# HGRN levels of a hybrid streaming encoder on one core: the masked copy bound behind both scalings, the first level's queries read side by side, one early pair's fourth weight sum on VectorE

## The chip, the cores and the metric

The kernel runs on one core of a Trainium2 chip. The metric is the device time of one execution, in microseconds, and the median over several runs is compared. A profile is of one execution, with times counted from the start of its span. The engines are named as the profile names them: PE (TensorE, matmuls, with PEld for its weight loads), DVE (VectorE), ACT (ScalarE), POOL (GpSimd) and SP (SyncE, which here only starts DMAs).

## The reference, cut to what matters

One inference step of one encoder layer, for 512 prompt frames and 32 frames of a running stream. A projection `proj = xn @ w_in` feeds two branches, an mLSTM with four heads and an HGRN2 with eight, and both are merged by gates and projected out. The change lies in the HGRN2 branch and in the projection that is computed beside it:

```
a = jnp.einsum('bhtc,bhtsc,bhsc->bhts', q, dec, k)      # dec = exp(g_t - g_s) for s <= t, per channel
o = jnp.einsum('bhtc,bhce->bhte', q * jnp.exp(g), S) + jnp.einsum('bhts,bhse->bhte', a, v)
```

The decay `dec` differs by channel c, so a plain matmul of q and k doesn't give `a`. The kernel computes it in levels.

## The kernel before

The frames are 544 columns (32 of the stream and 512 of the prompt), the 128 partitions are channels. The matrix products of the whole kernel are done by PE in three passes of rounded high and low parts, so each weight piece is cast by ACT (helper line L131) and its remainder is taken by DVE (L132). The projection's units come in pairs (class `Two`): seven products of 128x512 weight pieces and sums of pieces, in the manner of Strassen, in place of eight. The sums `s1`, `s2`, `s3`, `s4` of an early pair are made partly by DMAs that add into the tile (`s1`, `s3` in `begin`, L418 and L419, and `s4`, L476, all adding DMAs on POOL's queue), partly by DVE (L464). All sums `s1`, `s2`, `s4` of a pair live in one tile, called `ws` in the profile.

PE's order is written by hand: `Pump` hands out the pair products in steps of six matmuls (L501, tiles `d`), and `chain(h)`, which computes one HGRN head, says after each of its own pieces how many such steps follow (`STEPS`, 3 for most levels). The orders of DVE, ACT and POOL come from the tile framework's scheduler, which places each instruction by priority and by when it expects its inputs. Each engine then works its list strictly in order.

A head has seven levels, c = 1, 2, 4, ... 64. Tile `hkq` holds the head's keys `kk` and its queries `qq` side by side. At each level:

- ACT copies keys into `km`, a single buffer (L1640, later L1642), and for c under 16 saves some columns in `snap`.
- PE multiplies: two fp32 matmuls of 128 columns each into the PSUM tile `pl` (L1651, four instructions in the profile), at c = 16 three more columns' groups (L1659, L1661). The moving operand is read by `view`: runs of c columns, alternating between two places that are 288 + c columns apart.
- DVE scales half of the keys and half of the queries in place by decay products, in two instructions (L1675): the first scaling covers one half of the columns, the second the other. It then makes the next level's decay products (L1678, L1681) and copies the level's scores into `at` where a mask says so (L1682, COPY_PREDICATED).

The next level's `km` copy reads what the two scalings wrote, and the next level's matmuls read `km`. Nothing reads `at` before the head's last level is done.

Of the kernel before, what the change touches and what calls it, by code (L numbers as in the profile page):

```python
# [14 lines left out]
ALU = mybir.AluOpType  # L15
AX = mybir.AxisListType

P = 128
# [48 lines left out]
def hybrid_step(ctx: ExitStack, tc: tile.TileContext, a, o):  # L67
# [1442 lines left out]
    def view(t, off, dims):  # L1510
        base = t[:, 0:T]
        return bass.AP(base.tensor, base.offset + off, [list(base.ap[0])] + [list(d) for d in dims])
# [7 lines left out]
    def units():  # L1520


        def both(h):

            if "both" not in hs[h]:
                t = sp.tile([P, 2, SLOT], F32, tag="d", name=f"hkq{h}", bufs=2)
                hs[h].update(both=(t[:, 0], t[:, 1]), pair=t)
            return hs[h]["both"]

        def forget(h, raw):  # L1530
            lbc, lcc = lb[:, h : h + 1], lc[:, h : h + 1]
            tf, kk = eslot(f"tf{h}"), both(h)[0]
            for t, sign in ((tf, 1.0), (kk, -1.0)):
                S.activation(unrev(t), raw[:, :HB], AF.Sigmoid, scale=sign)
                S.activation(t[:, HB:T], raw[:, HB:T], AF.Sigmoid, scale=sign)
            S.activation(tf[:, :T], tf[:, :T], AF.Identity, scale=lcc, bias=lbc)
            S.mul(kk[:, :T], kk[:, :T], lcc)
            hs[h].update(tf=tf, kk=kk, kq=raw)

        def query(h, qq):  # L1540
            tf, kk, kq = (hs[h][k] for k in ("tf", "kk", "kq"))
            q0 = eslot(f"q0{h}")

            S.activation(unrev(q0), qq[:, :HB], AF.Sigmoid)
            S.activation(q0[:, HB:T], qq[:, HB:T], AF.Sigmoid)
            V.tensor_tensor(unrev(q0), unrev(q0), qq[:, :HB], ALU.mult)
            V.tensor_tensor(q0[:, HB:T], q0[:, HB:T], qq[:, HB:T], ALU.mult)
            V.tensor_tensor(qq[:, :T], q0[:, :T], tf[:, :T], ALU.mult)
            V.tensor_tensor(kq[:, :T], q0[:, :T], kk[:, :T], ALU.mult)
            hs[h].update(q0=q0, qq=qq)  # L1550

        def behind(h, then, t):

            if h:
                then(h, t)
            else:
                later.append(lambda: then(h, t))

        def value_tile(h):

            t = eslot(f"hi{h}")
            return t, (
                ((t[:, HB - 1 : HB - 1 - TH : -1], slice(0, TH)),),
                ((t[:, HB - 1 - TH :: -1], slice(0, HB - TH)), (t[:, HB:T], slice(HB - TH, TH))),
            )

        def value(h, t):
            hs[h]["ii"] = t

        def gate(h, t):  # L1570
            sg = slot(f"sg{h}")
            S.activation(sg[:, :T], t[:, :T], AF.Sigmoid)
            V.tensor_tensor(t[:, :T], t[:, :T], sg[:, :T], ALU.mult)
            hs[h]["gg"] = t

        def merge_a(f, t):
            gated[f] = S.activation(t[:, :T], t[:, :T], AF.Sigmoid)
            y = slot(f"ya{f}")[:, :T]
            nc.sync.dma_start(y, ya_d[f])
            V.tensor_tensor(y, y, t[:, :T], ALU.mult)  # L1580
            yas[f] = y

        def merge_b(f, t):
            S.activation(t[:, :T], t[:, :T], AF.Sigmoid)
            gbs[f] = t

        for h in range(HH):
            yield Two(
                [
                    (("q", h), 48 + h, lambda h=h: plain(both(h)[1]), lambda t, h=h: behind(h, query, t)),  # L1590
                    (
                        ("f", h),
                        56 + h,
                        lambda h=h: plain((slot if h else eslot)(f"kq{h}")),
                        lambda t, h=h: behind(h, forget, t),
                    ),
                ],
                h > 0,
                h == 0,
            )  # L1600
            yield Two(
                [
                    (("g", h), 72 + h, lambda h=h: plain(eslot(f"hg{h}")), lambda t, h=h: gate(h, t)),
                    (("i", h), 64 + h, lambda h=h: value_tile(h), lambda t, h=h: value(h, t)),
                ],
                True,
            )
        for f in range(0, KD, 2):
            for e in (
                pair("ga", f, 80 + f, lambda f: plain(eslot(f"ga{f}")), merge_a, True),  # L1610
                pair("gb", f, 88 + f, lambda f: plain(eslot(f"gb{f}")), merge_b, True),
            ):
                e.alone = True
                yield e
# [8 lines left out]
    def chain(h):  # L1623
# [10 lines left out]
        for li, c in enumerate(LEVELS):  # L1634
            smp = li == QUADS
            n = HB if smp else NA
            km = tp.tile([P, NA], F32, tag="vs", name=f"km{h}{c}", bufs=1)
            pump.behind = held[-1] if held else None
            with tc.high_priority():
                low = S.copy(  # L1640
                    km.rearrange("p (n j c) -> p n j c", j=2, c=c),
                    view(kk, HB, ((2 * c, NA // (2 * c)), (c - HB, 2), (1, c))),  # L1642
                )
                if li < QUADS:
                    S.copy(snap[:, :, li], hs[h]["pair"][:, :, csmp])
            held.append(low)
            yield STEPS[li]

            pn = paux(f"pl{h}{c}")
            for b in range(2):  # L1650
                PE.matmul(  # L1651
                    pn[:, 0, b * P : (b + 1) * P],
                    km[:, b * P : (b + 1) * P],
                    view(qq, b * P, ((2 * c, P // (2 * c)), (HB + c, 2), (1, c))),
                    start=True,
                    stop=True,
                )
            if smp:
                PE.matmul(pn[:, 0, NA:HB], kk[:, NA : NA + P], qq[:, csmp], start=True, stop=True)  # L1659
                ks, qs = (snap[:, i].rearrange("p l t -> p (l t)") for i in range(2))  # L1660
                PE.matmul(pn[:, 1, :P], ks, qs, start=True, stop=True)  # L1661
            nb, na = (HB if c < NS else NA) // (2 * c), NA // (2 * c)
            tb, ta = told[:, : 2 * nb], told[:, told.shape[-1] - 2 * na :]
            tn = ttmp[:, base : base + nb + na]
            sides = ((tb, 0, nb, 1, 0), (ta, HB, na, 0, nb))
            with tc.high_priority():
                for t, lo, m, first, _ in sides:

                    x = view(
                        kk, lo + first * c, ((qoff + (1 - 2 * first) * c, 2), (2 * c, m), (1, c))  # L1670
                    )
                    d = bass.AP(
                        t.tensor, t.offset + 1 - first, [list(t.ap[0]), [2 * first - 1, 2], [2, m], [0, c]]
                    )
                    V.tensor_tensor(x, x, d, ALU.mult)  # L1675
                if told.shape[-1] == 2 * (nb + na):
                    t = told.rearrange("p (n t) -> p n t", t=2)
                    V.tensor_tensor(tn, t[:, :, 0], t[:, :, 1], ALU.mult)  # L1678
                else:
                    for t, _, m, _, o_ in sides:  # L1680
                        V.tensor_tensor(tn[:, o_ : o_ + m], t[:, ::2], t[:, 1::2], ALU.mult)  # L1681
                V.copy_predicated(at[:, :n], lmask[:, li, :n], pn[:, 0, :n])  # L1682
                if smp:
                    for i in range(QUADS):
                        d = slice(i * NS, (i + 1) * NS)
                        V.copy_predicated(at[d, NA:HB], smask[d], pn[d, 1, d])
            base += nb + na
            if c == NS // 2:
                tsmp = tn[:, nb - 1 : nb]
            told = tn  # L1690
            if li == 0:

                yield 1
                pn = paux(f"pd{h}")
                for b, c_ in enumerate([c_ for c_, _, _ in chunks] + [slice(NA, NA + P)]):
                    PE.transpose(pn[:, b // NB, b % NB * P : (b % NB + 1) * P], kq[:, c_], ident)
                with tc.high_priority():
                    V.tensor_reduce(
                        dg, pn.rearrange("p a t -> p (a t)")[:, : 5 * P].rearrange("p (b t) -> p b t", t=P), AX.X, ALU.add
                    )  # L1700
            if li == (4 if h < HH - 1 else 6) and h:
                yield 1
                finish(h - 1)
# [328 lines left out]
```

## Time and profile before

| | |
|---|---|
| median of 3 runs | 1122.6 us (1119.49 to 1123.89) |
| the profiled execution: time, span | 1120.93 us, 1119.0 us |
| PE busy, PEld busy | 1108.0 us (99%), 1085.5 us (97%) |
| DVE busy, ACT busy, POOL busy | 896.4 us (80%), 669.9 us (60%), 167.8 us (15%) |
| granted TensorE clock | 1.000 |
| the HGRN heads' levels | 635.8 to 871.4 us |
| from one head's first level to the next one's | 30.7 us (729.41 to 760.09) |
| level matmuls, L1651 | 224 instructions, 37.8 us |
| level scalings L1675; masked copies L1682; km copies L1640 | 96 records, 40.7 us; 56, 25.2 us; 56, 24.0 us |

A row of the timeline has the start, the duration, the engine, the line, the instruction with its tiles, and in brackets the idle time in front of it with what ended that. Neighbours on one engine overlap a little in the records: the next DVE instruction starts some 0.08 us before the end that is shown for the one ahead, so a time from start to start is what an instruction costs its engine.

### The profile page before, as it was taken

To read this page: it belongs to the slowest core of one execution; us is meant where nothing else is said; L and a number is where in the kernel's file an instruction comes from. 1 tells how busy PE (TensorE), PEld (TensorE's weight loads), DVE (VectorE), ACT (ScalarE), POOL (GpSimd) and SP (SyncE) were. 2 spreads that over 40 slices of the span, in tenths; PEclk is the share of its full clock that TensorE was granted. 3 is DMA by queue.
4 is the path that set the end of the run, shared out by engine and by line. 5 is a ranking of instruction groups with operands and counts; after the bars stand their busy time and mean duration, and the time that the engine had idled before them with its cause. 6 is when DMAs were issued, how large, how long until landed. Compare 5 with 4: busy or idle time off the path is not lost.

```text
span 1119.0 us, 23773 instructions
## 1 busy us (share of the span) xinstructions
PE 1108.0 (99%) x8733; PEld 1085.5 (97%) x8733; DVE 896.4 (80%) x2040; ACT 669.9 (60%) x1506; POOL 167.8 (15%) x308
## 2 busy tenths in 40 slices
PE   9999999999999999999999999999999999999998
PEld 9889999999999999999999999999999999999998
DVE  6898988676896786976888699999999977654485
ACT  6767446754666555664655476777676667333462
POOL 7223010100020000200010123232222210000000
PEclk9999999999999999999999999999999999999999
DMA  6133314332353133541767655666665684332743
GB/s 230 57 113 118 124 57 163 117 95 96 128 175 141 57 119 124 164 164 60 240 166 252 179 133 133 147 137 144 150 157 144 160 223 157 109 105 71 263 153 118
DMA packets 90139, 157.94 MB, mean 141 GB/s; under 512 B 10148, under 2 KB 17828, under 8 KB 90024
## 3 DMA queue, kind: packets, MB, share of 16 engines
q1 hardware_dynamic: 80352, 139.33, 37.8%
q0 software_dynamic: 8784, 15.99, 9.0%
q8 instruction: 68, 1.11, 0.4%
q10 hardware_dynamic: 888, 1.12, 0.3%
q14 instruction: 47, 0.39, 0.1%
HBM read 131.49 MB, written 24.91 MB: 140 GB/s over the span
## 4 chain that ended last, share of the span: by engine, by line
PE 92%; DVE 4%; DMA 1%; ACT 1%; issue 1%; SPq 0%; POOL 0%; ACTq 0%; POOLq 0%; DVEq 0%
PE d L501 36%; PE ya L166 9%; PE pg L1879 4%; PE yb L166 4%; PE q L166 4%; PE o L166 4%; PE C L927 4%; PE k L166 4%; PE sc L887 3%; PE nm L1102 3%; PE pl L1651 2%; PE u L286 2%; PE vp L1410 2%; PE ple L166 1%; PE d L386 1%; DMA ws<-in_w_in 1%
## 5 line engine op out<-in xcount | busy, mean ns | idle before, releaser
L419 POOL DMA_DIRECT2D ws<-in_w_in x46 | 40.4, 884 | 228.4 <-DVE hkq L1675 22.2
L515 ACT COPY t<-d 128x272 f32<-128x272 f32 x126 | 47.7, 379 | 8.8 <-PE d L501 8.7
L1675 DVE TENSOR_TENSOR hkq<-hkq,q 128x288 f32<-128x288 f32 (+1 forms) x96 | 40.7, 430 | 2.5 <-PE pl L1659 0.9
L1651 PE MATMUL pl<-hkq,km 128*128 128x128 f32 x224 | 37.8, 291 | 1.3 <-ACT km L1640 1.1
L650 DVE SCALAR_TENSOR_TENSOR cv<-ub,vec,cv 128x547 f32<-128x547 f32 x48 | 37.5, 782 | 0.4
L1651 PEld LDWEIGHTS pl<-hkq,km 128*128 128x128 f32 x224 | 31.2, 189 | 3.0 <-ACT km L1640 2.7
L1640 ACT COPY km<-hkq 128x256 f32<-128x256 f32 x56 | 24.0, 428 | 16.5 <-DVE hkq L1675 7.4
L1036 DVE SCALAR_TENSOR_TENSOR c<-c,wi,Cs 128x258 f32<-128x258 f32 x32 | 15.3, 479 | 18.5 <-PE Cs L1034 18.1
L939 ACT COPY Co<-C 128x258 f32<-128x258 f32 x30 | 9.8, 378 | 30.7 <-PE C L927 28.4
L1187 DVE TENSOR_TENSOR y<-ya,y 128x272 f32<-128x272 f32 x48 | 18.8, 433 | 8.8 <-PE ya L166 8.7
L1682 DVE COPY_PREDICATED at<-lmask,pl 128x256 f32<-128x256 uint8 (+1 forms) x56 | 25.2, 449 | 0.1
L1113 ACT COPY y<-nm 128x516 f32<-128x516 f32 x16 | 9.4, 590 | 22.7 <-PE nm L1102 22.6
L642 POOL COPY uo<-ub 128x3 f32<-128x3 f32 x16 | 17.5, 1092 | 34.5 <-DVE ub L524 26.5
L476 POOL DMA_DIRECT2D ws<-in_w_in x15 | 15.5, 1032 | 33.9 <-DVE ws272l L132 24.9
L1619 POOL TENSOR_SCALAR_AFFINE_SELECT aa<-at 128x128 f32<-128x128 f32 x32 | 19.2, 682 | 8.0 <-DVE at L1682 8.0
L1090 DVE BATCH_NORM_STATS2 bs<-y 128x6 f32<-128x512 f32 (+1 forms) x20 | 13.8, 690 | 8.0 <-ACT y L1113 7.8
L826 POOL COPY vsm<-vt 128x96 f32<-128x96 f32 x12 | 6.2, 515 | 88.9 <-DVE vt L522 45.4
L1102 PE MATMUL nm<-vhl,sh 128*128 128x258 f32 x112 | 18.4, 286 | 0.6 <-ACT y L1113 0.6
L1866 DVE TENSOR_TENSOR h<-o,h 128x272 f32<-128x272 f32 x16 | 6.3, 436 | 14.5 <-PE o L166 14.5
L1781 ACT ACTIVATE osq<-kq 128x128 f32<-128x128 f32 x32 | 9.8, 305 | 12.4 <-DVE kq L1776 12.1
L901 ACT CAST sh<-dm 128x512 fp32r<-128x512 f32 (+3 forms) x16 | 7.3, 458 | 16.3 <-DVE dm L895 16.3
L1102 PEld LDWEIGHTS nm<-vhl,sh 128*128 128x128 f32 x112 | 15.4, 190 | 1.2 <-ACT y L1113 0.8
(4498 smaller groups left out, 4985.2 us busy)
## 6 DMA issues: line engine op xcount, KB each, us to landing
ws<-in_w_in POOLq DMA_DIRECT2D x61, 256.0 KB, 4.6
ws<-in_w_in SPq DMA_DIRECT2D x46, 256.0 KB, 3.5
ya_d<-y SPq DMA_DIRECT2D x32, 272.0 KB, 2.3
y<-ya_d SPq DMA_DIRECT2D x24, 272.0 KB, 3.8
c<-in_C SPq DMA_DIRECT2D x16, 258.0 KB, 3.6
out_Cs<-c SPq DMA_DIRECT2D x16, 258.0 KB, 2.7
out_Cp<-Co SPq DMA_DIRECT2D x12, 258.0 KB, 2.5
x<-in_xT SPq DMA_DIRECT2D x8, 272.5 KB, 5.1
```

The source lines that it names most:

```text
L166: PE.matmul(both[b][:m, :TH], part(w, off + k * step, m, x), xx[:, half(b)], start=(k == 0 and j == 0), stop=(k == n - 1 and j == 2),)
L419: G.dma_start(t, w_in[u][:, i * WP : (i + 1) * WP], accum_op=ALU.add)
L501: PE.matmul(ps, ww[:, c], xx, start=(start and k == 0 and j == 0), stop=end, skip_group_check=not start,)
L515: self.kept = S.copy(t, ps)
L650: V.scalar_tensor_tensor(cv[:, :547], ub[:, j : j + 547], vcol(V_CW + 4 * ft + j), cv[:, :547], ALU.mult, ALU.add)
L887: PE.matmul(pn[:, 0, :n], ks[f][x][:, j * P : (j + 1) * P], qs[f][y][:, NS + j * P : T], start=(f == 0 and i == 0), stop=(f == KH - 1 and ...
L927: PE.matmul(pn[g][:, :VH], kw[b][x][:, f * P : (f + 1) * P], vv[b][y][:, g * VH : (g + 1) * VH], start=(b == 0 and j == 0), stop=(b == NB ...
L1102: PE.matmul(pn[:, g, :VH], st[j][x][:, (i - j) * P : (i - j + 1) * P], vv[j][y][:, g * VH : (g + 1) * VH], start=(j == 0 and q == 0), stop ...
L1651: PE.matmul(pn[:, 0, b * P : (b + 1) * P], km[:, b * P : (b + 1) * P], view(qq, b * P, ((2 * c, P // (2 * c)), (HB + c, 2), (1, c))), star ...
L1675: V.tensor_tensor(x, x, d, ALU.mult)
L1682: V.copy_predicated(at[:, :n], lmask[:, li, :n], pn[:, 0, :n])
L1879: PE.matmul(ps, part(w, k * P, P, x), xx[:, c], start=(k == 0 and j == 0), stop=(k == KD - 1 and j == 2))
```

## The change

It has three parts. In `units()`, the first pair of head 1 (queries and forget gate, units 49 and 57) gets `alone = True`, by which its fourth sum `s4` is made by a DVE addition (L464) and not by an adding DMA from POOL (L476). In `chain(h)`, at the level c = 1, the moving operand is read as 64 columns two apart in one place and then 64 two apart in the other, and the result is written into `pl` two columns apart, so that it stands in the same order as before. And the masked copy L1682 gets an ordering edge behind the level's second scaling.

```
@@ units()
-            yield Two(
+            first = Two(
...
                 h > 0,
                 h == 0,
             )
+            first.alone = h == 1
+            yield first
@@ chain(h)
             for b in range(2):
-                PE.matmul(
-                    pn[:, 0, b * P : (b + 1) * P],
-                    km[:, b * P : (b + 1) * P],
-                    view(qq, b * P, ((2 * c, P // (2 * c)), (HB + c, 2), (1, c))),
-                    start=True,
-                    stop=True,
-                )
+                out, dims = pn[:, 0, b * P : (b + 1) * P], ((2 * c, P // (2 * c)), (HB + c, 2), (1, c))
+                if c == 1:
+                    out, dims = out.rearrange("p (i s) -> p s i", s=2), (dims[1], dims[0])
+                PE.matmul(out, km[:, b * P : (b + 1) * P], view(qq, b * P, dims), start=True, stop=True)
...
-                    V.tensor_tensor(x, x, d, ALU.mult)
+                    scaled = V.tensor_tensor(x, x, d, ALU.mult)
...
-                V.copy_predicated(at[:, :n], lmask[:, li, :n], pn[:, 0, :n])
+                with tc.issue_after(scaled.ins):
+                    V.copy_predicated(at[:, :n], lmask[:, li, :n], pn[:, 0, :n])
```

PE's list stays as it was, but for the form of the c = 1 matmuls. DVE's and ACT's lists are laid out anew by the scheduler through all eight heads. The profile's lines of the unchanged code shift by one or two: the scaling L1675 becomes L1674, the `km` copy L1640 becomes L1642, `snap` L1645 becomes L1647, L1678 becomes L1677.

DVE, head 3, level c = 4 (`pl_10491` is its score tile, `hkq_9773` the head's keys and queries, `ws_10272` the sum tile of a gate pair in the pump, L524 and L183 other work). Before:

```order
L524 SCALAR_TENSOR_TENSOR kq_10248<-d_10246,t_10474 128x272
L1675 TENSOR_TENSOR hkq_9773<-hkq_9773,q_10123 128x2x36x4
L1682 COPY_PREDICATED at_10364<-lmask,pl_10491 128x256
L1675 TENSOR_TENSOR hkq_9773<-hkq_9773,q_10123 128x2x32x4
L183 SCALAR_TENSOR_TENSOR rsq_u<-rsq_u,hv 128x5
L464 TENSOR_TENSOR ws_10272<-ws_10272,wi76r_9982 128x512
```

The same place in the changed kernel:

```order
L524 SCALAR_TENSOR_TENSOR kq_10248<-d_10246,t_10474 128x272
L1674 TENSOR_TENSOR hkq_9773<-hkq_9773,q_10123 128x2x36x4
L183 SCALAR_TENSOR_TENSOR rsq_u<-rsq_u,hv 128x5
L464 TENSOR_TENSOR ws_10272<-ws_10272,wi76r_9982 128x512
L1674 TENSOR_TENSOR hkq_9773<-hkq_9773,q_10123 128x2x32x4
L1682 COPY_PREDICATED at_10364<-lmask,pl_10491 128x256
```

The masked copy has left the place between the two scalings, and a five-column step and a weight sum of 128x512 have taken it. At this level the heads 1 to 7 read alike.

ACT, head 3, from the `km` copy of c = 8 (`km_10498`) to that of c = 16 (`km_10545`); `ws276h` is the cast of the sum that L464 made. Before:

```order
L1640 COPY km_10498<-hkq_9773 128x256
L1645 COPY snap<-hkq_9773 128x2x32
L131 CAST ws276h<-ws_10272 128x512
L1535 ACTIVATE tf_10560<-kq_10248 128x256
L131 CAST ws376h<-ws_10275 128x512
L1640 COPY km_10545<-hkq_9773 128x256
L526 ACTIVATE kq_10248<-d_10245 128x272
```

The same stretch in the changed kernel:

```order
L131 CAST ws276h<-ws_10272 128x512
L1642 COPY km_10498<-hkq_9773 128x256
L1647 COPY snap<-hkq_9773 128x2x32
L131 CAST ws376h<-ws_10275 128x512
L1535 ACTIVATE tf_10560<-kq_10248 128x256
L526 ACTIVATE kq_10248<-d_10245 128x272
L1642 COPY km_10545<-hkq_9773 128x256
```

The `km` copy of c = 8 now stands behind the cast of the sum, and that of c = 16 behind L526, which reads a pair product that PE must have finished.

DVE, head 3, level c = 32 (`pl_10647`); L1548 and L1549 make the next head's queries. Before:

```order
L1548 TENSOR_TENSOR hkq_10247<-q_10597,tf_10560 128x544
L1675 TENSOR_TENSOR hkq_9773<-hkq_9773,q_10123 128x2x4x32
L1682 COPY_PREDICATED at_10364<-lmask,pl_10647 128x256
L1675 TENSOR_TENSOR hkq_9773<-hkq_9773,q_10123 128x2x4x32
L1549 TENSOR_TENSOR kq_10248<-q_10597,hkq_10247 128x544
```

And in the changed kernel:

```order
L1548 TENSOR_TENSOR hkq_10247<-q_10597,tf_10560 128x544
L1674 TENSOR_TENSOR hkq_9773<-hkq_9773,q_10123 128x2x4x32
L1549 TENSOR_TENSOR kq_10248<-q_10597,hkq_10247 128x544
L1674 TENSOR_TENSOR hkq_9773<-hkq_9773,q_10123 128x2x4x32
L1677 TENSOR_TENSOR q_10597<-tf_10560 128x272
L1682 COPY_PREDICATED at_10364<-lmask,pl_10647 128x256
```

Here the 544-column product L1549 stands between the scalings. So it is in the heads 1 to 6.

## The prediction

> **What bounds the kernel now.** I read the page first: the engines' shares and the chain.
>
> ```profile
> PE 1108.0 (99%) x8733; PEld 1085.5 (97%) x8733; DVE 896.4 (80%) x2040; ACT 669.9 (60%) x1506; POOL 167.8 (15%) x308
> PE 92%; DVE 4%; DMA 1%; ACT 1%; issue 1%; SPq 0%; POOL 0%; ACTq 0%; POOLq 0%; DVEq 0%
> ```
>
> PE is busy for 99% of the span and carries 92% of the chain. Only two things can move the end: what PE itself does, and the moments when it waits. DVE at 80% looks harmless, but the change lies in one stage, so next come the windows there (columns: length, then busy us of PE, PEld, DVE, ACT, POOL).
>
> ```profile
> 700.00:800.00 100.00, 100.00 (x811) 99.22 (x810) 97.45 (x277) 72.10 (x203) 28.46 (x40) 1.00 0.65 149
> ```
>
> Among the HGRN heads PE is full and DVE too, at 97%: a list of work in strict order with hardly a gap. What is put ahead of something there delays it by its full length. The waits of PE for the `km` copies, from the view of waits, say how much there is to win:
>
> ```profile
> PEld pl L1651 <- ACT km L1640: 2.7, 6, 0.9
> ```
>
> Six waits, 2.7 us in all. Together with a cheaper first level (below, at most 1.8 us) the whole change has some 4.5 us to win, 0.4% of the time. Differences within 0.5% (5.6 us) are about what the measurement can't tell from none, so a clear gain is nearly excluded from the start.
>
> **The first level's queries.** The timeline of PE in head 3: the level matmuls of c = 1, c = 2 and c = 32, each with the next two matmuls.
>
> ```profile
> 729.41 0.83 PE L1651 MATMUL pl<-hkq,km 128*128 128x128 f32 x4
> 729.94 0.43 PE L501 MATMUL d<-xfh,ws252h 128*128 128x272 f32 x1
> 730.21 0.29 PE L501 MATMUL d<-xfl,ws252h 128*128 128x272 f32 x1
> ...
> 733.62 0.64 PE L1651 MATMUL pl<-hkq,km 128*128 128x128 f32 x4
> 734.01 0.38 PE L501 MATMUL d<-xfh,ws352h 128*128 128x272 f32 x1
> 734.23 0.29 PE L501 MATMUL d<-xfl,ws352h 128*128 128x272 f32 x1
> ...
> 746.31 0.61 PE L1651 MATMUL pl<-hkq,km 128*128 128x128 f32 x4
> 746.68 0.37 PE L501 MATMUL d<-xfh,ws176h 128*128 128x272 f32 x1
> 746.89 0.28 PE L501 MATMUL d<-xfl,ws176h 128*128 128x272 f32 x1
> ```
>
> From the first start to the second matmul behind it c = 1 takes 0.80 us, c = 2 0.61 and c = 32 0.58. Runs of one column, alternating between two far places, cost 0.19 us over runs of two. The new reading steps by two columns within one place. Its nearest row is c = 2, so I take a gain of 0.19 a head, 1.5 us in eight. No row shows a PSUM result written two columns apart. The ends are a gain as far as c = 32 (0.22 a head, 1.8 us) and a loss of the same size, if the writing costs more than the reading gives.
>
> [...]
>
> **The moved copy.** On DVE the copy leaves the place between the scalings, which would bring the second scaling forward by 0.34 us, and the list shows something longer in its place. Head 3, from c = 4 to the matmuls of c = 8, DVE, ACT and PE:
>
> ```profile
> 737.29 0.45 DVE L1675 TENSOR_TENSOR hkq<-hkq,q 128x288 f32<-128x288 f32 x1
> 737.66 0.44 DVE L1682 COPY_PREDICATED at<-lmask,pl 128x256 f32<-128x256 uint8 x1
> 738.00 0.42 DVE L1675 TENSOR_TENSOR hkq<-hkq,q 128x256 f32<-128x256 f32 x1
> 738.33 0.16 DVE L183 SCALAR_TENSOR_TENSOR rsq_u<-rsq_u,hv 128x5 f32<-128x5 f32 x1
> 738.40 0.68 DVE L464 TENSOR_TENSOR ws<-ws,wi76r 128x512 f32<-128x512 f32 x1
> 738.50 0.41 ACT L1640 COPY km<-hkq 128x256 f32<-128x256 f32 x1 [0.29 <-DVE rsq_u L183]
> 739.12 0.62 ACT L131 CAST ws276h<-ws 128x512 fp32r<-128x512 f32 x1
> 739.14 0.64 PE L1651 MATMUL pl<-hkq,km 128*128 128x128 f32 x4
> 739.64 0.41 ACT L1535 ACTIVATE tf<-kq 128x256 f32<-128x256 f32 x1
> ```
>
> Now: first scaling 737.29, `km` starts 0.08 behind the second, ends at 738.91, and PE needs it at 739.14, 0.23 later. After: first scaling at 737.29 again (the list ahead of it is the same), L183 at 737.66, L464 at 737.73 to 738.41, second scaling from 738.33 to 738.75. On ACT the cast of that sum now stands ahead of `km`: it starts 0.04 behind L464, at 738.45, and holds ACT for 0.52 (739.12 to 739.64), so `km` runs from 738.97 to 739.38. PE starts 0.05 behind a `km` copy that it waits for, at 739.43: 0.29 late. A level that starts out of a wait is also longer, as head 0 shows:
>
> ```profile
> 646.85 0.75 PE L1651 MATMUL pl<-hkq,km 128*128 128x128 f32 x4 [0.28 <-ACT km L1640]
> 647.34 0.38 PE L501 MATMUL d<-xfh,wa2249h 128*128 128x272 f32 x1
> ```
>
> 0.49 us to the next matmul, against 0.39 at c = 2 above: 0.10 more. At c = 8 PE loses 0.39.
>
> From c = 8 to c = 16 the `km` copy now stands behind L526, which waits for a pair product:
>
> ```profile
> 741.01 0.29 PE L501 MATMUL d<-xfh,wa2252l 128*128 128x272 f32 x1
> 741.12 0.41 ACT L1640 COPY km<-hkq 128x256 f32<-128x256 f32 x1 [0.55 <-DVE hr L184]
> 741.43 0.39 ACT L526 ACTIVATE kq<-d 128x272 f32<-128x272 f32 x1
> 741.89 0.61 PE L1651 MATMUL pl<-hkq,km 128*128 128x128 f32 x4
> ```
>
> The product ends at 741.30, with the shift of 0.39 at 741.69; L526 follows 0.04 later, at 741.73, `km` 0.31 behind it, 742.04 to 742.45, PE at 742.50. It would have been there at 741.89 + 0.39 = 742.28. It loses 0.22 and, as above, 0.10 for the restart: 0.32.
>
> From c = 16 to c = 64, DVE's rows around both levels, and the end:
>
> ```profile
> 743.00 0.45 DVE L1675 TENSOR_TENSOR hkq<-hkq,q 128x288 f32<-128x288 f32 x1
> ...
> 747.41 0.42 DVE L1675 TENSOR_TENSOR hkq<-hkq,q 128x256 f32<-128x256 f32 x1
> 748.08 0.42 DVE L1675 TENSOR_TENSOR hkq<-hkq,q 128x256 f32<-128x256 f32 x1
> 748.41 0.72 DVE L1549 TENSOR_TENSOR kq<-q,hkq 128x544 f32<-128x544 f32 x1
> 748.59 0.41 ACT L1640 COPY km<-hkq 128x256 f32<-128x256 f32 x1 [0.38 <-DVE hkq L1675]
> 749.05 0.71 PE L1651 MATMUL pl<-hkq,km 128*128 128x128 f32 x4
> ```
>
> DVE has no gap from 743.00 to here, so only what is in the list counts. L1549 enters ahead of the second scaling of c = 32 (0.72, less the overlap of 0.08), a 128-column step enters at c = 16 (some 0.2), and the copy between the scalings of c = 32 leaves (0.33 of the 0.67 from 747.41 to 748.08): 0.5 later. Here the slack is nothing: `km` ends at 749.00 and PE starts at 749.05. The restart at c = 16 covers none of it, since DVE's first scaling waits for those matmuls. I take 0.48 at c = 64. At c = 1 a 512-column remainder enters in the same way, some 0.3 more than the copy, and is hidden there: the row below ends at 731.95, and the c = 2 matmuls come at 733.62. At c = 2 the list leaves the scalings side by side.
>
> ```profile
> 731.50 0.45 ACT L1640 COPY km<-hkq 128x256 f32<-128x256 f32 x1
> 687.71 0.52 PEld L1651 LDWEIGHTS pl<-hkq,km 128*128 128x128 f32 x4 [0.36 <-ACT km L1640]
> ```
>
> Heads 2 to 6: 0.39 + 0.32 + 0.48 = 1.2 us each, 6.0. Head 1 already waits 0.36 at c = 64 (the second row), so 0.9. Head 7 has a second sum between its c = 8 scalings and a product and an addition between those of c = 16; by the same reckoning 1.3. Sum 8.2 us lost.
>
> **The fourth sum.** Head 0's rows:
>
> ```profile
> 635.02 1.18 POOL L476 DMA_DIRECT2D ws<-in_w_in  x1
> 642.60 0.62 ACT L131 CAST ws449h<-ws 128x512 fp32r<-128x512 f32 x1 [3.07 <-DMA ws<-in_w_in]
> 643.12 0.40 ACT L1640 COPY km<-hkq 128x256 f32<-128x256 f32 x1
> 643.58 0.74 PE L1651 MATMUL pl<-hkq,km 128*128 128x128 f32 x4 [0.67 <-ACT km L1640]
> ```
>
> The adding DMA is issued at 635.02 and its sum is cast only at 642.60; `km` of c = 4 stands behind that cast, and PE waits (0.9 with its restart). A DVE addition takes 0.68 (L464 above); it stands ahead of head 0's first level, and PE needs its product only some levels on. POOL's queue loses one DMA, SP's keeps its loads. The 0.9 goes. But at c = 8 head 0 gets the same cast ahead of `km`, and its present wait there grows by some 0.3. At c = 64 it gains back 0.1. I take a gain of 0.7.
>
> **The sum.** 8.2 - 1.5 - 0.7 = 6.0 us on the profiled execution's 1120.9: 1126.9. That execution lies 1.7 below the median of 1122.6 and inside the runs' range; on the median it is 1128.6. I forecast 1127.5. With the ends of the first level's price (gain 1.8, loss 1.8) it is 1127 to 1131, and if the small waits at c = 8 and 16 come out half as long, 1125.
>
> **The rivals.**
>
> The strided PSUM write costs PE more than the reading gives (0.2 more per head than now): 8.2 - 0.7 + 1.8 = 9.3, so 1130.5. For it speaks that the write loses its contiguity; against it, that no row shows a price. [...]
>
> The delays are mostly taken up by slack: L526 or the cast don't hold `km` where I put them, since ACT is only 72% busy, and c = 64 alone waits: 7 x 0.48 - 1.5 - 0.7 = 1.2, so 1123. Against it stands the strict order of ACT's list.
>
> The other side: the second scaling isn't what delays `km`, because DVE comes to it early. Decisive is the slack at c = 8: if `km` there starts less than 0.23 later than now, and the c = 32 scaling comes less than 0.05 later, no new wait arises. Then head 0's waits go (2.1 with restarts, of the 2.7 above) and the first level gives 1.8: 3.9 less, 1118. For it, the copy does leave the path at every level; against it, L464 is 0.24 longer than the copy from start to start, and DVE is 97% busy.
>
> **How the numbers follow.** Forecast 0.50, PSUM write 0.17, slack 0.18, other side 0.15. Slower by over 0.5% (above 1128.2) are the PSUM case and some 0.6 of the forecast: 0.47. Faster by over 0.5% (under 1117) is out of reach of all but a part of the last: 0.04. The rest, 0.49, is no difference. The range of 1119.5 to 1131.5 leaves out half of the other side and a tail above the PSUM case. The forecast's own range is 1125 to 1130.
>
> **What would show it.** In heads 2 to 6: `km` of c = 8 directly behind the cast of `ws2..h`, `km` of c = 16 behind L526, L1549 between the scalings of c = 32, PE waiting for `km` at c = 8, 16 and 64, and 31.7 us from one head's first level to the next instead of 30.7. At c = 1: 0.39 instead of 0.53 us from the level's start to the next matmul; 0.6 or more would be the PSUM case. In head 0: no 3 us of ACT in front of `ws449h`. I am wrong if PE reaches c = 8 without a wait, or if DVE waits in those heads where I have it busy.

## The result and the profile after

| | before | after |
|---|---|---|
| median | 1122.46 us (7 runs) | 1126.2 us (7 runs) |
| ratio, 95% interval | | 1.005 [1.0039, 1.0062] |
| the profiled execution: time, span | 1120.93 us, 1119.0 us | 1126.2 us, 1124.4 us |

By the ratio the changed kernel is 5.6 us slower; the two medians alone are 3.7 us apart. The page after, the engines and the chain:

```profile
PE 1109.7 (99%) x8733; PEld 1084.2 (96%) x8733; DVE 898.6 (80%) x2041; ACT 670.6 (60%) x1506; POOL 169.9 (15%) x307
PE 82%; DVE 11%; ACT 3%; DMA 2%; issue 2%; SPq 0%; ACTq 0%; DVEq 0%
```

The busy times hardly differ. The chain does: DVE's share went from 4% to 11%, PE's from 92% to 82%. PE now waits more often for work that DVE releases. In the view of waits, the row that had 6 waits and 2.7 us before:

```profile
PEld pl L1656 <- ACT km L1642: 8.4, 24, 0.7
```

The window from 700 to 800 us tells only a part of it (before: PE 100.00, PEld 99.22, DVE 97.45, and 811 matmul records):

```profile
700.00:800.00 100.00, 98.97 (x795) 96.99 (x794) 96.44 (x273) 70.73 (x196) 28.56 (x39) 1.00 0.63 145
```

Where the 5.4 us between the two spans lie, by the starts of the c = 1 matmuls and of `ht` in head 7:

| stretch | before | after | difference |
|---|---|---|---|
| to head 0, c = 1 | 635.78 | 634.82 | -0.96 |
| head 0 | 31.99 | 30.61 | -1.38 |
| heads 1 to 6 | 184.33 | 187.96 | +3.63 |
| head 7 to `ht` | 20.58 | 23.13 | +2.55 |
| from there to the end | 246.32 | 247.88 | +1.56 |

The first row is code that the change hardly touches. It comes to between 634.4 and 637.1 in the profiles of this study, on both sides of the change, so it doesn't count for it. Of the last row, 1.4 us lie behind PE's last matmul, in the output's last transfers, and this part goes with the kernel: in the four profiles with the old order of the masked copies (before, e1, e3, e6) 3.1 to 3.2 us follow PE's last matmul, in the nine others 4.0 to 4.9. SP's last eight output DMAs, before and then after (the duration runs from the first issue to the last), and one queue in the view of DMAs of the changed kernel from 1114 us on (packets, MB, share):

```profile
1111.20 3.87 SPq L1903 DMA_DIRECT2D out_y<-h  x8
1115.18 5.24 SPq L1903 DMA_DIRECT2D out_y<-h  x8
q8 instruction: 1, 0.02, 0.8%
```

In the changed kernel's profile the queue that the page calls `instruction` moves one packet there, and SP's eight issues take 5.24 us; in the profile of before it moves none from 1111 us on, and they take 3.87. The page counts 23815 instructions after and 23773 before. What the longer issues have to do with the packet or with the program's length, no run shows.

Now the places. The first level of head 3, PE's timeline:

```profile
728.29 0.64 PE L1656 MATMUL pl<-hkq,km 128*128 128x128 f32 x4
728.67 0.38 PE L501 MATMUL d<-xfh,ws252h 128*128 128x272 f32 x1
728.89 0.29 PE L501 MATMUL d<-xfl,ws252h 128*128 128x272 f32 x1
```

0.60 us from the start to the second matmul behind it, 0.80 before. From c = 4 to the matmuls of c = 8 in head 3, DVE, ACT and PE:

```profile
736.01 0.45 DVE L1674 TENSOR_TENSOR hkq<-hkq,q 128x288 f32<-128x288 f32 x1
736.45 0.68 DVE L464 TENSOR_TENSOR ws<-ws,wi76r 128x512 f32<-128x512 f32 x1
737.05 0.42 DVE L1674 TENSOR_TENSOR hkq<-hkq,q 128x256 f32<-128x256 f32 x1
737.17 0.62 ACT L131 CAST ws276h<-ws 128x512 fp32r<-128x512 f32 x1 [0.24 <-DVE ws L464]
737.69 0.40 ACT L1642 COPY km<-hkq 128x256 f32<-128x256 f32 x1
738.15 0.75 PE L1656 MATMUL pl<-hkq,km 128*128 128x128 f32 x4
738.64 0.38 PE L501 MATMUL d<-xfh,wa2252h 128*128 128x272 f32 x1
```

The second scaling starts 1.04 behind the first instead of 0.71, the `km` copy stands directly behind the cast, and PE starts 0.06 behind its end. The start to the next matmul takes 0.49, not 0.39: the level begins out of a wait. The rest of the head, c = 8 to c = 64:

```profile
740.45 0.40 ACT L526 ACTIVATE kq<-d 128x272 f32<-128x272 f32 x1 [1.37 <-PE d L501]
740.74 0.40 ACT L1642 COPY km<-hkq 128x256 f32<-128x256 f32 x1
741.19 0.71 PE L1656 MATMUL pl<-hkq,km 128*128 128x128 f32 x4
742.15 0.46 DVE L1674 TENSOR_TENSOR hkq<-hkq,q 128x288 f32<-128x288 f32 x1 [0.37 <-PE pl L1658]
...
747.15 0.72 DVE L1549 TENSOR_TENSOR kq<-q,hkq 128x544 f32<-128x544 f32 x1
747.79 0.42 DVE L1674 TENSOR_TENSOR hkq<-hkq,q 128x256 f32<-128x256 f32 x1
748.30 0.41 ACT L1642 COPY km<-hkq 128x256 f32<-128x256 f32 x1 [0.67 <-DVE hkq L1674]
748.76 0.71 PE L1656 MATMUL pl<-hkq,km 128*128 128x128 f32 x4 [0.15 <-ACT km L1642]
```

ACT stood idle for 1.37 us ahead of L526, with the `km` copy queued behind it; and DVE waited 0.37 us for PE in front of the first scaling of c = 16. Two more places differ. Before, PE's timeline in head 3 behind c = 64, and at the end of head 7:

```profile
752.34 0.29 PE L501 MATMUL d<-xl,wa1253h 128*128 128x272 f32 x1
752.59 0.39 PE L501 MATMUL d<-xh,wa1253l 128*128 128x272 f32 x1
752.82 0.29 PE L501 MATMUL d<-xh,wa1253h 128*128 128x272 f32 x1
...
872.68 0.63 PE L1727 MATMUL ht<-ident,hi 128*128 128x128 f32 x4
```

The same places after:

```profile
752.05 0.29 PE L501 MATMUL d<-xl,wa1253h 128*128 128x272 f32 x1
752.17 0.29 PE L501 MATMUL d<-xh,wa1253l 128*128 128x272 f32 x1
752.30 0.29 PE L501 MATMUL d<-xh,wa1253h 128*128 128x272 f32 x1
...
876.52 0.63 PE L1727 MATMUL ht<-ident,hi 128*128 128x128 f32 x4 [1.30 <-DVE at L1682]
```

Before, PE lost 0.23 us at the first use of the remainder `wa1253l` (0.25 and 0.23 between starts, where 0.125 is usual). After, that remainder comes earlier on DVE and the loss is gone. And in head 7 there is a new wait of 1.30 us: the transposes `ht` need a PSUM buffer of the pool that `pl` uses, which has two, and the masked copy of c = 64 gives it back late.

### The profile page after: what moved, and what is told of

It reads as the page before. It is cut to its first block, busy times and chain, and to the rows that moved or that the text cites. A ratio compares the mean times of both kernels' runs of the same rounds, so it can differ in the third digit from the quotient of the medians.

```text
span 1124.4 us, 23815 instructions
## 1 busy us (share of the span) xinstructions
PE 1109.7 (99%) x8733; PEld 1084.2 (96%) x8733; DVE 898.6 (80%) x2041; ACT 670.6 (60%) x1506; POOL 169.9 (15%) x307
## 4 chain that ended last, share of the span: by engine, by line
PE 82%; DVE 11%; ACT 3%; DMA 2%; issue 2%; SPq 0%; ACTq 0%; DVEq 0%
PE d L501 29%; PE ya L166 8%; PE pg L1879 4%; PE yb L166 4%; PE q L166 4%; PE o L166 4%; PE C L927 4%; PE k L166 4%; PE sc L887 3%; PE nm L1102 3%; PE vp L1410 2%; PE u L286 2%; DVE hkq L1674 2%; PE pl L1656 2%; PE ple L166 1%
## 5 line engine op out<-in xcount | busy, mean ns | idle before, releaser
L1674 DVE TENSOR_TENSOR hkq<-hkq,q 128x288 f32<-128x288 f32 (+1 forms) x96 | 40.8, 432 | 5.3 <-PE pl L1658 3.7
L1642 ACT COPY km<-hkq 128x256 f32<-128x256 f32 x56 | 23.7, 423 | 11.3 <-DVE hkq L1674 8.2
L1682 DVE COPY_PREDICATED at<-lmask,pl 128x256 f32<-128x256 uint8 (+1 forms) x56 | 25.0, 446 | 0.1
L476 POOL DMA_DIRECT2D ws<-in_w_in x14 | 16.2, 1156 | 24.0 <-DVE ws272l L132 23.9
L1853 DVE TENSOR_TENSOR gb<-yb,gb 128x272 f32<-128x272 f32 x16 | 6.3, 436 | 13.0 <-PE yb L166 13.0
```

The costliest lines, as they stand in the source:

```text
L1674: scaled = V.tensor_tensor(x, x, d, ALU.mult)
```

## The experiments

From a level's start to the next level's, mean of the heads 1 to 6, in us (the last column reaches to the next head's c = 1):

| kernel | 1 to 2 | 2 to 4 | 4 to 8 | 8 to 16 | 16 to 32 | 32 to 64 | 64 to 1 |
|---|---|---|---|---|---|---|---|
| before | 4.22 | 2.75 | 2.74 | 2.75 | 4.44 | 2.77 | 11.05 |
| after | 4.03 | 2.76 | 3.06 | 3.05 | 4.54 | 3.07 | 10.82 |
| e1, queries alone | 4.02 | 2.76 | 2.74 | 2.76 | 4.44 | 2.77 | 11.05 |
| e2, copy alone | 4.22 | 2.76 | 3.06 | 3.04 | 4.53 | 3.08 | 10.82 |
| e4, late copy of 64 | 4.02 | 2.76 | 2.74 | 2.79 | 4.44 | 2.83 | 10.81 |
| e5, sum behind scaling | 4.03 | 2.76 | 2.74 | 2.79 | 4.53 | 2.94 | 11.05 |
| e8, edge at 32 only | 4.03 | 2.76 | 2.74 | 2.75 | 4.44 | 3.08 | 10.82 |

**e1, the queries alone.** The kernel before with the new reading and writing at c = 1, and nothing else:

```
+                if c == 1:
+                    out, dims = out.rearrange("p (i s) -> p s i", s=2), (dims[1], dims[0])
```

> The kernel before with one part of the change, the c = 1 queries read side by side and their result written two columns apart. Theory 1 (the loss comes from the copy's ordering edge, the other two parts gain): each head gains the 0.19 us that the changed kernel shows at c = 1 (0.60 us against 0.79 from the level's start to the second matmul behind it), 1.5 us in eight: ratio 0.9987, and no list of DVE or ACT differs. Rival (the write two columns apart costs PE time elsewhere, as a slower write-out that the level's rows don't show): no gain or up to 1.8 us slower, ratio 1.000 to 1.0016.

Measured: 0.9988 [0.9979, 0.9996], 1.3 us less. In the table only the first column moves, by 0.20. The part gains what its rows say.

**e2, the copy alone.** The kernel before with the ordering edge, and nothing else:

```
+                with tc.issue_after(scaled.ins):
+                    V.copy_predicated(at[:, :n], lmask[:, li, :n], pn[:, 0, :n])
```

> The kernel before with one part of the change, the masked copy's ordering edge behind the second scaling. Theory 1: the whole loss and more of it than the changed kernel shows, since both gains are missing: the changed kernel's heads 1 to 7 are 6.2 us longer than before, and 1.3 of gain at c = 1 stands against that, so the edge alone costs 7.5 us there; head 0 keeps its wait of 0.9 at c = 4 and waits somewhat longer at c = 8 (0.3): 7.8 us, ratio 1.0069. Rival (the loss is from the strided write or from the moved DMA, and the edge only moves waits about): under 3 us, ratio below 1.0027.

Measured: 1.0069 [1.0057, 1.0081], 7.7 us. All of the changed kernel's longer spacings are there, its wait at `ht` (1.31 us) and its longer end (1.4 us more than before behind PE's last matmul). The loss is the edge's.

**e3, the queries and the sum.** The changed kernel without the edge.

```
-                with tc.issue_after(scaled.ins):
-                    V.copy_predicated(at[:, :n], lmask[:, li, :n], pn[:, 0, :n])
+                V.copy_predicated(at[:, :n], lmask[:, li, :n], pn[:, 0, :n])
```

> The changed kernel without the masked copy's ordering edge: the c = 1 queries side by side and the fourth sum on VectorE. Theory 1: 1.5 us from c = 1 and 0.9 from head 0's wait at c = 4, 2.4 us less than before, ratio 0.9979, and 6 to 8 us less than the changed kernel. Rival (the edge is not what costs): like the changed kernel, ratio 1.003 or more. Second rival (the sum's DVE addition delays head 0 elsewhere): not better than the queries alone, ratio 0.9987.

Measured: 0.9984 [0.9974, 0.9994]. Against the changed kernel it is 7.4 us less, as the theory has it. Against e1 it is 0.4 us less, within the uncertainty of both: the fourth sum's gain of 0.9 can't be seen. e1's profile says why. It still has the adding DMA; POOL's, ACT's and PE's rows at head 0's c = 4:

```profile
633.21 1.18 POOL L476 DMA_DIRECT2D ws<-in_w_in  x1
639.40 0.63 ACT L131 CAST ws449h<-ws 128x512 fp32r<-128x512 f32 x1 [1.35 <-DMA ws<-in_w_in]
641.28 0.64 PE L1655 MATMUL pl<-hkq,km 128*128 128x128 f32 x4
```

Here the cast comes 6.19 us behind the DMA's issue, 7.58 in the profile of before (6.38 in e2), and PE doesn't wait at c = 4. From issue to cast these profiles differ by up to 1.39 us; the 0.9 was one execution's.

**e4, a late copy of the last level.** As e3, with the masked copy of c = 64 at normal priority in heads 0 to 6, to make the remainder `wa1253l` early without the edge.

```
-                V.copy_predicated(at[:, :n], lmask[:, li, :n], pn[:, 0, :n])
+                if not (c == 64 and h < HH - 1):
+                    V.copy_predicated(at[:, :n], lmask[:, li, :n], pn[:, 0, :n])
...
+            if c == 64 and h < HH - 1:
+                V.copy_predicated(at[:, :n], lmask[:, li, :n], pn[:, 0, :n])
```

> The queries and the fourth sum as changed, no ordering edge, and the masked copy of the last level c = 64 at normal priority in heads 0 to 6, so that on DVE it stands behind the remainders L132 that follow it today. Theory 1 with what the traces showed beside it (the changed kernel has no wait of PE at the remainder of wa1253 and its like, 0.22 a head, because that remainder comes earlier on DVE): 0.2 to 0.4 in each of the heads 1 to 6 on top of the 2.4 us, 1.2 to 2.4 more, ratio 0.9958 to 0.9968. Rival (what hurts in late copies is that they keep the PSUM buffer of pl, of which there are two, as at the end of head 7 in the changed kernel where PE waits 1.3 us behind the copy): PE waits behind this copy at the next user of the buffer, up to 1.3 a head, ratio 0.999 to 1.006.

Measured: 0.998 [0.9971, 0.9988]. The last column falls by 0.24 in each of the heads, and no wait for the buffer arises there. The runs show less than the forecast: 0.4 us below e3 where 1.2 to 2.4 were expected; the uncertainty of that difference, some 1.5 us from the two intervals, reaches into it. In e4's profile the heads 1 to 6 together are 1.1 us shorter than in e3's, and 0.9 us are lost again behind PE's last matmul. Heads 4 and 0 wait again for `km` copies behind casts of other sums that adding DMAs bring late (0.20 and 0.49 us).

**e5, the sum behind the scaling.** The changed kernel with one more edge, so that the 128x512 sum no longer enters between the scalings of c = 4.

```
+    def edge():
+        last = scalings[0]
+        return tc.issue_after(last.ins) if last is not None else nullcontext()
...
-                V.tensor_tensor(t, x, y, ALU.add)
+                with edge():
+                    V.tensor_tensor(t, x, y, ALU.add)
...
+                scalings[0] = scaled
```

> The changed kernel with one ordering edge more: the weight sum of L464 is queued on VectorE behind the latest second scaling, so that at c = 4 only the five-column L183 stands between the scalings. The copy stays behind both. ACT's km copy of c = 8 then stands ahead of the cast of that sum and that of c = 16 ahead of L526. Theory 1 (not the edge itself costs, but the longer step that takes the copy's place): c = 4 to 8 falls from 3.06 us back to 2.75, c = 8 to 16 from 3.05 to 2.75 to 2.80, since a 512-column remainder still stands between the scalings of c = 8 and the slack there, 0.36, just covers its 0.33; c = 32 to 64 stays at 2.9 to 3.07, with L1548 between the scalings of c = 32. Heads 1 to 6 take 30.55 to 30.75 us each in place of 31.3: 3.5 to 4.5 us less than the changed kernel in all, ratio to before 1.000 to 1.0018. Rival (the late masked copies cost by holding the two pl buffers): the spacings stay at 3.05, ratio 1.004 or more.

The spacings came out as expected: 2.74, 2.79, 2.94. With the edge in place and the copy behind both scalings, c = 4 to 8 loses nothing when only the five-column step stands between them. From c = 8 to 16 the loss falls from 0.30 to 0.04, though a 512-column remainder stands between those scalings as in the changed kernel (1.05 us from start to start in both); here `km` no longer stands behind the step that is L526 in the changed kernel. But the time is 1.0034 [1.0021, 1.0047], beyond the forecast. From the timeline of PE and the windows at the end of head 7:

```profile
873.40 1.08 PE L1734 MATMUL ht<-ident,hi 128*128 128x128 f32 x4 [2.20 <-DVE at L1689]
```

```profile
873.00:874.00 1.00, 0.60 (x3) 0.63 (x4) 1.00 (x4) 0.00 (x0) 0.61 (x3) 0.58 0.86 158
874.00:875.00 1.00, 1.00 (x7) 1.00 (x6) 1.00 (x3) 0.26 (x1) 0.86 (x2) 0.50 0.94 214
875.00:876.00 1.00, 1.00 (x6) 1.00 (x6) 0.97 (x2) 1.00 (x5) 0.00 (x0) 0.50 0.97 302
876.00:877.00 1.00, 1.00 (x8) 1.00 (x7) 0.13 (x1) 0.37 (x2) 0.00 (x0) 0.72 0.96 347
```

The wait for the buffer has grown to 2.20 us, and from 873.16 us, just before its end, the granted clock (third number from the end) is 0.50 for 3.4 us; PE's matmuls of 272 columns start 0.22 to 0.23 us apart there, 0.12 to 0.13 ahead of the pause. By the clock that is another 1.7 us, an estimate. The end behind PE's last matmul, 4.8 us, takes 1.6 more than before.

**e6, wide steps in PSUM.** As e3, and the results of the other levels are written in steps as well, up to 64 columns apart.

```
+                else:
+                    out = out.rearrange("p (i s) -> p s i", s={2: 2, 4: 4, 8: 8, 16: 16, 32: 32, 64: 64}[c])
```

> The queries and the fourth sum as changed, no ordering edge, and the two matmuls of each level c > 1 also write their result in strides: 2 columns of fp32 apart at c = 2, 4 at c = 4, 8, 16, 32, and 64 columns (256 bytes) at c = 64. The scores inside a tile then stand in another order than the reference's, so the results differ; the amount of work doesn't. Theory 1 (a strided write is free at these sizes): from a level's start to the second matmul behind it 0.58 to 0.61 us at c = 2 to 8 and 32, as in the kernels with plain writes, and from 2.74 to 2.77 us from level to level; span as without the strides, 1115 to 1119. Rival (a non-contiguous result slows matmuls): 0.2 us or more at each of the levels, more at the wider steps, 0.2 x 6 levels x 8 heads = 10 us or more, span above 1126.

Measured, in one execution: span 1116.8, and level to level 4.02, 2.76, 2.74, 2.76, 4.44, 2.82, 11.05. At c = 32, with 128 bytes between neighbours of the result:

```profile
744.40 0.61 PE L1658 MATMUL pl<-hkq,km 128*128 128x128 f32 x4
744.76 0.37 PE L501 MATMUL d<-xfh,ws176h 128*128 128x272 f32 x1
744.97 0.29 PE L501 MATMUL d<-xfl,ws176h 128*128 128x272 f32 x1
```

0.57 us, as with a plain write (0.58 before). At c = 64, with 256 bytes, it is 0.66 us, as before. The rival of the PSUM write is out.

**e7, no edge at the last level.** The changed kernel with

```
-                with tc.issue_after(scaled.ins):
+                with tc.issue_after(scaled.ins) if c < 64 else nullcontext():
```

> The changed kernel with the masked copy's ordering edge at all levels but the last, c = 64. The copy of c = 64 stands between that level's scalings in head 7 again and ahead of the remainder ws488l. If the late copy keeps the pl buffer that ht of head 7 needs: the wait of PE at ht in head 7, 1.3 us there in the changed kernel, goes, and from head 7's first level to ht's matmuls it gets 1.3 us shorter; heads 1 to 6 keep c = 4 to 8, 8 to 16 and 32 to 64 at 3.05 us, so this explains none of their loss. Span 1.3 us below the changed kernel's, 1123. Rival (ht waits for something else): the wait stays.

```profile
874.73 0.63 PE L1727 MATMUL ht<-ident,hi 128*128 128x128 f32 x4
```

The wait at `ht` is gone: from head 7's c = 64 to `ht` 1.95 us, 3.31 after, 1.93 before. The spacings of the heads 1 to 6 stay at 3.06, 3.04 and 3.08. The span of this one execution is 1123.0. So there are two losses among the heads: `km` behind late scalings, and in head 7 the buffer.

**e8, the edge at c = 32 only.** As e3, with `if c == 32` in the place of `if c < 64`.

> The queries and the fourth sum as changed, and the ordering edge at the level c = 32 alone. On DVE L1549 (0.64 from start to start) takes the copy's place (0.34) between the scalings of c = 32, and the rest of the list stays as before in heads 1 to 6. Theory 1: c = 32 to 64 takes 2.77 + 0.30 + 0.10 for the restart less the 0.05 of slack, 3.05 to 3.15 us, all other spacings as without the edge (2.75, 2.74, 2.75, 4.44). Rival (the forecast's 0.48 at c = 64 was right and the changed kernel got something back by its earlier c = 16): here, with c = 16 as before, 2.77 + 0.30 only if L1549 alone counts, 3.25 if more of the list does. Rival (late buffers): no change at 32 to 64, since the copy is later by 0.3 us only.

32 to 64 takes 3.08, with no other level longer: L1549 in the copy's place costs the 0.31 by itself. The gain of 0.23 behind c = 64 comes with it, which wasn't expected; three quarters of the loss come back there. DVE's rows give the reason: a part of the decay products (L1677) has come ahead of that level's scalings, and the remainder `wa1253l` starts 2.52 us behind the level's matmuls, as in the changed kernel, and not 2.81 as before. The span of this one execution is 1120.0, of which an estimated 1.65 is lost to the clock (last section).

**e9, e5 without the edge at the last level.** The edit of e7 in the kernel of e5.

> The kernel with the sum queued behind the scaling (e5), with the masked copy's ordering edge at all levels but the last, c = 64. That kernel's heads were 1.3 us shorter than before's, but it measured 1.0034; its profile has PE waiting 2.20 us at ht of head 7 for the copy of c = 64, which keeps one of the two pl buffers, and then a granted clock of 0.5 for 3.3 us, 1.65 us lost. Theory (the late copy of the last level and the clock behind the long pause cost 3.9 us there): the wait at ht goes, the clock stays 1.0 from 870 to 880 us, ratio to before 0.9985 to 1.0005, 3 to 4.5 us below the former 1125.0. Rival (the rest of its loss is spread, from adding DMAs that land late): 1.3 to 2 us below, ratio 1.0015 to 1.0025.

Measured: 1.0009 [0.9999, 1.002], 2.8 us below e5. The clock stays 1.0 there. The wait at `ht` shrank from 2.20 to 0.85 us and did not go: in these two kernels a product of 544 columns (0.72 us in the row) has come ahead of the scalings of c = 64 in head 7, which start 1.73 us behind the level's matmuls here, 1.70 in e5 and 1.02 in the changed kernel. By its profile (heads 0 to 6 together 1.5 us shorter than before, 0.83 lost at `ht`, 1.3 behind PE's last matmul) 1.0005 would follow, which lies within the interval.

**e10, the late copy of c = 64 in head 7 too.** The kernel of e4 without `and h < HH - 1`.

> The kernel with the late copy of c = 64 in heads 0 to 6 (e4, ratio 0.998), with that copy late in head 7 too: there it stands behind the remainder of wa1282, the second scaling, L524 and the remainder of wa2288, some 1.9 us later. Theory (the copy keeps the buffer that ht of head 7 needs, and a pause of PE of more than 1.7 to 1.9 us halves the granted clock for 3.3 us): PE waits 1.7 to 2.0 us at ht of head 7; all heads before as in e4; ratio 0.9995 if the clock stays, 1.001 if it halves. Rival (a late copy is harmless, the waits seen at ht come from elsewhere): 0.998 again.

The 1.7 and 1.9 us of this theory are pauses of two profiles: one of 1.68 us in e5 (up to 78.95 us), with a granted clock of 1.00 from 78 to 83 us, and one of 1.89 us in e8, behind which the clock was 0.50 for 3.41 us (last section).

Measured: 1.0009 [0.9997, 1.0021], 3.3 us above e4. The rows of PE's timeline, and of the windows there:

```profile
79.85 0.74 PE L166 MATMUL k<-cs0h,wk000h 128*128 128x272 f32 x2 [2.07 <-DVE z L686]
...
872.14 0.63 PE L1729 MATMUL ht<-ident,hi 128*128 128x128 f32 x4 [2.00 <-DVE at L1688]
```

```profile
79.00:84.00 5.00, 4.15 (x31) 3.99 (x32) 4.97 (x12) 4.08 (x9) 0.85 (x1) 1.00 0.00 0
871.00:877.00 6.00, 4.86 (x41) 4.89 (x42) 4.24 (x10) 4.09 (x12) 1.47 (x4) 1.00 0.66 217
```

PE waits 2.00 us for the buffer, as forecast from DVE's list. The clock did not fall behind it in this execution. Of the twelve executions five have a mean granted clock of 0.997 or 0.998 and take 2.0 us more on average than the other seven. Those seven are 2.2 us above e4's executions with a clock of 0.999 or 1.000, so the wait accounts for some 2 of the 3.3 us, and the lower clock of the five for some 0.7 more. Where in these the clock fell is not recorded.

**e11, both early sums.** e4, and the gate pair of head 1 gets `alone = True` as well.

```
-            yield Two(
+            second = Two(
...
+            second.alone = h == 1
+            yield second
```

> The kernel with the late copy of c = 64 in heads 0 to 6 (e4, ratio 0.998), with the fourth sum of head 1's gate pair (ws473 in the profile) on VectorE too, in place of an adding DMA. In the profiles of the kernels without the edge, head 0 waits 0.3 to 0.8 us at c = 64 behind the cast of that sum. Theory: that wait goes in head 0, some 0.5 us, ratio 0.9975; all other heads unchanged. Rival (the addition delays head 0's own steps on VectorE by 0.6 as much as it saves): 0.998 or more, a wait at c = 32 or 64 of head 0 with DVE as its cause.

Measured: 0.9976 [0.9966, 0.9986], the fastest version: 2.7 us less than before and, by the two ratios, 8.3 less than the changed kernel. It can't be told from e4 by its time. In its profile the cast of `ws473h` no longer waits for a DMA; the gap in front of head 0's c = 64 is 0.42 us from start to start, 1.06 in e3 and 0.13 where nothing is late. But it is 0.46 in e10, which keeps that DMA, so this gain too can be one execution's.

## Why the prediction came out where it did

1127.5 us was forecast and 1126.2 measured. The sum was 8.2 - 1.5 - 0.7 = 6.0; the parts alone measure 7.7 (e2), 1.3 (e1) and 0.4 (e3 against e1, unresolved), 6.0 again, and the whole 5.6. That the sum fits so well is partly luck, as the terms show. In the profiles the heads are 4.8 us longer, not 6.0, and 1.4 us come from the end, for which the forecast had no term; e2's 7.7 holds 1.4 of the same kind.

- *The first level* was right: 0.19 us a head forecast from the row of c = 2, 0.19 measured. The PSUM rival had 0.17 of the chance. No run shows the loss of 0.2 us a head (1.8 us in all) that its sum takes for the strided write: e1, with that write at c = 1, gains 0.20 a head, and in e6 it is 0.57 us from a level's start to the second matmul behind it with 128 bytes between neighbours of the result (0.58 before) and 0.66 with 256 bytes (0.66 before).
- *The moved copy, c = 8 and 16* were right in mechanism and size: at c = 8 0.29 late was forecast and 0.32 measured, with the restart of 0.10, and from c = 8 to 16 0.32 forecast, 0.30 measured. In e5 the sum is gone from between the scalings of c = 4 and `km` of c = 16 stands ahead of L526's step; 0.32 and 0.26 of these go.
- *The moved copy, c = 64* is the term that was too large: 0.48 forecast, 0.30 measured. The list did grow by the 0.5 that was reckoned (from the first scaling of c = 16 to the end of the second of c = 32: 5.50 us before, 6.06 after). What failed is "the restart at c = 16 covers none of it". Before, that first scaling started 1.11 us behind the level's matmuls, because DVE was still busy with its list; after, the remainder that stood ahead of it had moved between the scalings of c = 8, and DVE waited for PE (0.37, the row above) and started 0.96 behind. 0.15 and the restart's 0.10 were given back. This is the sign named beforehand: DVE waits where it was taken to be busy.
- *Behind c = 64* nothing was forecast, and 0.23 a head came back: the remainder `wa1253l` starts 0.29 us earlier on DVE, because decay products that stood ahead of it were made before the level's scalings, and PE's two short gaps there were not read, since the profile lists no wait for them. With that, a head lost 0.8 in e2 instead of 1.2, and the forecast's 31.7 us from head to head was 31.3.
- *Head 7* was too small: 1.3 forecast, 2.75 in e2. Nearly all of the missing 1.4 is the wait at `ht` (1.31). It was said of the kernel that nothing reads `at` before the head's last level is done, and so the copy was taken to be free to move; but the copy reads `pl`, and who needs `pl`'s buffer next was not asked.
- *The fourth sum* rested on one execution. The changed kernel's profile has no wait at c = 4, as forecast; but e1 keeps the DMA and has none either. Whether the part gains is open; 0.7 is within what was measured, and so is nothing.

The rivals on the other end fell at c = 8. The slack of 0.23 there, by which the other side was to be decided, is used up because something longer fills the place; and ACT's idle time takes nothing up, since `km` is queued behind the instruction that waits (L526, 1.37 us idle ahead of it).

## What to carry over

An ordering edge that takes one instruction out of a place leaves the place open, and the scheduler fills it with whatever is ready: read what stands there afterwards, and what it holds up on the next engine, before counting the gain. An instruction that only consumes still owns its input's buffer, so the next user of that buffer belongs to the cost of moving it (here 1.30 us at `ht`). Compare two profiles behind the last matmul too: 1.4 us of the difference lie there, far from the code that was changed. And a wait for a transfer that is read off one execution can be that execution's alone (6.19, 6.38 and 7.58 us from issue to cast in three profiles here): ask a second profile before it becomes a term of the sum.

## What was not expected of the hardware

Behind two pauses of PE the granted clock was 0.50 for 3.4 us. In e5 it was the 2.20 us above; in e8, a wait near the start of the program, which takes 1.09 to 2.07 us in nine of the thirteen profiles and under 0.7 in the others. PE's timeline and windows of e8:

```profile
79.36 0.74 PE L166 MATMUL k<-cs0h,wk000h 128*128 128x272 f32 x2 [1.89 <-DVE z L686]
```

```profile
79.00:84.00 5.00, 4.64 (x23) 4.48 (x24) 5.00 (x12) 4.29 (x8) 0.85 (x1) 0.67 0.00 0
77.25:80.66 3.41, 1.52 (x10) 1.14 (x9) 3.35 (x7) 2.46 (x5) 0.25 (x1) 1.00 0.00 0
80.66:84.07 3.41, 3.41 (x17) 3.41 (x16) 3.41 (x9) 3.39 (x7) 0.85 (x1) 0.50 0.00 0
```

At 0.50 two matmuls of PE take 0.45 us there, 0.25 ahead of the pause. A mean of 0.67 over 5 us is, by the clock, an estimated 1.65 us lost, or 3.3 us at 0.50. So a pause of 1.89 us was followed by it, and pauses of 2.00 and 2.07 (e10), with a clock of 1.00 in the windows above, were not: here the length alone doesn't decide. In the 3.41 us ahead of the fall, as long as the clock then stood at 0.50, PE was busy for 1.52 us in e8 and for 1.45 in e5 (from 869.75 to 873.16 us). Stretches of that length with PE busy for 1.34 and 1.41 us lie around the two pauses of e10, where the clock stayed at 1.00. So PE's busy time in such a stretch doesn't decide either. What does, no run shows.
